# Contrast adjustment: stores issued from GpSimd's queue instead of ScalarE's

## Chip, cores, metric

One core of one Trainium2 chip. The time is the device time of one execution in microseconds (us); lower is better. Each tensor is 16 x 3 images of 512 x 512 float32 numbers, 50.33 MB, read once and written once.

## The reference

```python
mean = np.mean(x, axis=(2, 3), keepdims=True)
return np.clip(mean + factor * (x - mean), 0, 1).astype(np.float32)   # factor = 1.5
```

So the kernel computes, for each image, the sum of its pixels, and then `clip(factor * x + (1 - factor) * mean, 0, 1)`.

## The kernel before

Twelve tiles of 128 rows x 8192 columns (4.19 MB, four images each) go through a ring of six buffers in SBUF, in place. The parts that matter here:

```python
P, ROW, BUFS, SHORT, SUM = 128, 8192, 6, 2048, 4352
FIRST = (SHORT, ROW - SHORT)
# ... pools, constants, blockw: a 128 x 128 matrix that adds up the 32 rows of an image ...

def load(t, c0=0, c1=ROW, n=1):          # n tiles, columns c0 to c1, on SyncE's queue
    # ...
    nc.sync.dma_start(out=ring[:, b : b + n, c0:c1], in_=src)

def compute(t):
    xt = ring[:, t % BUFS, :]
    own = sums[:, 2 * t : 2 * t + 2]
    nc.vector.tensor_reduce(out=own[:, 0:1], in_=xt[:, 0:SUM], ...)                 # L81
    nc.scalar.activation(out=junk, in_=xt[:, SUM:ROW], func=Act.Copy, accum_out=own[:, 1:2])  # L84
    shift = bias[:, t : t + 1]
    nc.tensor.matmul(shift, blockw, own[:, 1:2], start=True, stop=False)            # L86
    nc.tensor.matmul(shift, blockw, own[:, 0:1], start=False, stop=True)            # L87
    c = 0
    for n in FIRST if t == 0 else [ROW]:
        part = xt[:, c : c + n]
        nc.vector.tensor_scalar(out=part, in0=part, scalar1=factor, scalar2=shift, ...)   # L91: x * factor + shift
        nc.vector.tensor_scalar(out=part, in0=part, scalar1=0.0, scalar2=1.0, ...)        # L94: clip
        store(t, c, c + n)
        c += n

def store(t, c0, c1):
    nc.scalar.dma_start(out=dram(out_f, t, c0, c1), in_=ring[:, t % BUFS, c0:c1])   # L101

load(0, c1=SHORT); load(0, c0=SHORT); load(1); load(2, n=2); load(4, n=2)
for t in range(n_tiles):
    compute(t)
    if t + BUFS < n_tiles:
        load(t + BUFS)          # waits until the store of tile t has landed
```

Of the kernel before, what the change touches and what calls it, by code (L numbers as in the profile page):

```python
# [1 line left out]

# [4 lines left out]


P = 128  # L10
ROW = 8192
BUFS = 6
SHORT = 2048
FIRST = (SHORT, ROW - SHORT)
SUM = 4352


@with_exitstack
def kernel(
    ctx: ExitStack,  # L20
    tc: tile.TileContext,
    x: bass.AP,
    factor: float,
    out: bass.AP,
):



    nc = tc.nc
    f32 = mybir.dt.float32  # L30
    Alu = mybir.AluOpType
    Act = mybir.ActivationFunctionType

    B, C, H, W = x.shape
    n_img, n_pix = B * C, H * W
    ppi = n_pix // ROW
    per_tile = P // ppi
    n_tiles = n_img // per_tile
    assert ppi * ROW == n_pix and per_tile * n_tiles == n_img

    factor = float(factor)
    wconst = (1.0 - factor) / float(n_pix)

    x_f = x.rearrange("b c h w -> (b c h w)")
    out_f = out.rearrange("b c h w -> (b c h w)")

    def dram(ap, t, c0=0, c1=ROW):
        return bass.AP(tensor=ap.tensor, offset=t * P * ROW + c0, ap=[[ROW, P], [1, c1 - c0]])

    consts = ctx.enter_context(tc.tile_pool(name="consts", bufs=1))  # L50
    xpool = ctx.enter_context(tc.tile_pool(name="xpool", bufs=1))
    small = ctx.enter_context(tc.tile_pool(name="small", bufs=1))
    psum = ctx.enter_context(tc.tile_pool(name="psum", bufs=1, space=bass.MemoryType.PSUM))


    sums = small.tile([P, 2 * n_tiles], f32, name="sums")
    junk = small.tile([P, ROW - SUM], f32, name="junk")
    bias = psum.tile([P, n_tiles], f32, name="bias")

    blockw = consts.tile([P, P], f32, name="blockw")  # L60
    nc.gpsimd.memset(blockw, 0.0)  # L61
    for a in range(0, P, ppi):
        nc.gpsimd.memset(blockw[a : a + ppi, a : a + ppi], wconst)  # L63


    ring = xpool.tile([P, BUFS, ROW], f32, name="ring")

    def load(t, c0=0, c1=ROW, n=1):

        b = t % BUFS  # L70
        src = bass.AP(
            tensor=x_f.tensor,
            offset=t * P * ROW + c0,
            ap=[[ROW, P], [P * ROW, n], [1, c1 - c0]],
# [6 lines that stand above are left out]
        nc.vector.tensor_reduce(  # L81
            out=own[:, 0:1], in_=xt[:, 0:SUM], axis=mybir.AxisListType.X, op=Alu.add
# [8 lines that stand above are left out]
            nc.vector.tensor_scalar(  # L91
                out=part, in0=part, scalar1=factor, scalar2=shift, op0=Alu.mult, op1=Alu.add
            )
            nc.vector.tensor_scalar(  # L94
                out=part, in0=part, scalar1=0.0, scalar2=1.0, op0=Alu.max, op1=Alu.min
            )
            store(t, c, c + n)
            c += n

    def store(t, c0, c1):  # L100
        nc.scalar.dma_start(out=dram(out_f, t, c0, c1), in_=ring[:, t % BUFS, c0:c1])  # L101

    with tc.manual_schedule():
        load(0, c1=SHORT)
        load(0, c0=SHORT)
        load(1)
        load(2, n=2)
        load(4, n=2)
# [3 lines that stand above are left out]
                load(t + BUFS)  # L112


# [1 line left out]
_INS = ['x', 'factor']  # L116
_OUTS = [((16, 3, 512, 512), 'float32')]

_NUMBERS = {'factor': 1.5}


# [26 lines left out]
```

## Time and profile before

| | before |
|---|---|
| time, median | 239.31 us (239.30 to 239.37, 3 runs) |
| span of the profiled run | 237.3 us |
| DMA queues, share of 16 engines | loads 49.7%, stores 49.2% |
| VectorE / ScalarE / GpSimd busy | 163.1 / 43.2 / 0.9 us |
| HBM traffic over the span | 424 GB/s |

How to read it: an engine's busy time is set against the span, and the two queue shares add up, because both queues feed the same 16 DMA engines. Here they add up to 98.9%: the DMA engines are the bound, and VectorE at 69% is not. The rows themselves are shown in the prediction.

### The profile page before, as it was taken

The page shows a single profiled execution, that of the slowest core. Times are in us where ns is not written, and L with a number is a line of the kernel's source. Part 1 is how long each engine was busy: PE and PEld are TensorE (multiplying, and loading weights), DVE is VectorE, ACT ScalarE, POOL GpSimd, SP SyncE. Part 2 cuts the span into 40 slices and gives each one's busy share as a digit, 9 for nine tenths or more (in the row PEclk, how much of TensorE's full clock was granted, in tenths as well). Part 3 has the DMA queues.
Part 4 walks back from the last instruction along what each step waited for, and adds up shares of the span by engine and source line. Part 5 has one row for each costly group of instructions (what it writes and reads, how often), then busy time and mean ns, then how long its engine had stood idle before and what let it go on. Part 6 is the DMA issues. An engine that isn't in the chain of part 4 may idle for free.

```text
span 237.3 us, 285 instructions
## 1 busy us (share of the span) xinstructions
PE 14.1 (6%) x48; PEld 12.0 (5%) x48; DVE 163.1 (69%) x38; ACT 43.2 (18%) x25; POOL 0.9 (0%) x9
## 2 busy tenths in 40 slices
PE   0010010001010001010010100100100100010000
PEld 0010010001010001010010100100100100010000
DVE  0079989048989328999989898891892795687000
ACT  2050230041050023050320504101400500500000
POOL 1000000000000000000000000000000000000000
DMA  7999999999999999999999999999999999999996
GB/s 297 410 442 442 421 442 359 456 439 441 442 436 414 403 431 442 442 442 442 436 442 436 414 409 425 442 442 442 442 436 442 436 420 403 425 442 442 442 442 265
DMA packets 3712, 100.66 MB, mean 424 GB/s; under 512 B 384, under 2 KB 384, under 8 KB 384
## 3 DMA queue, kind: packets, MB, share of 16 engines
q1 hardware_dynamic: 1840, 50.33, 49.7%
q10 hardware_dynamic: 1872, 50.33, 49.2%
HBM read 50.33 MB, written 50.33 MB: 424 GB/s over the span
## 4 chain that ended last, share of the span: by engine, by line
DMA 57%; DVE 29%; another core or an unknown queue 3%; PE 1%; SPq 1%; issue 0%; DVEq 0%
DMA ring<-in_x_dram 41%; DMA out_dram<-ring 16%; DVE sums L81 10%; DVE ring L91 9%; DVE ring L94 9%; PE bias L87 1%; SPq L76 1%; DVEq L91 0%
## 5 line engine op out<-in xcount | busy, mean ns | idle before, releaser
L81 DVE TENSOR_REDUCE sums<-ring 128x1 f32<-128x4352 f32 x12 | 56.2, 4683 | 45.7 <-DMA ring<-in_x_dram 45.7
L84 ACT ACTIVATE junk<-ring 128x3840 f32<-128x3840 f32 x12 | 40.8, 3403 | 163.3 <-DMA ring<-in_x_dram 107.5
L91 DVE TENSOR_SCALAR ring<-ring,bias 128x8192 f32<-128x8192 f32 (+2 forms) x13 | 54.1, 4163 | 8.9 <-PE bias L87 7.4
L94 DVE TENSOR_SCALAR ring<-ring 128x8192 f32<-128x8192 f32 (+2 forms) x13 | 53.3, 4099 | 0.4
L86 PE MATMUL bias<-sums,blockw 128*128 128x1 f32 x24 | 7.0, 361 | 190.8 <-ACT junk L84 190.8
L86 PEld LDWEIGHTS bias<-sums,blockw 128*128 128x128 f32 x24 | 6.0, 312 | 191.7 <-ACT junk L84 175.2
L87 PE MATMUL bias<-sums,blockw 128*128 128x1 f32 x24 | 7.0, 363 | 4.3 <-DVE sums L81 3.9
L87 PEld LDWEIGHTS bias<-sums,blockw 128*128 128x128 f32 x24 | 6.0, 311 | 5.3 <-DVE sums L81 5.0
L84 ACT ACTIVATION_READ_ACCUMULATOR junk<-ring 128x1 f32 x12 | 2.2, 186 | 0.0
L84 ACT ACT_TABLE_LOAD x1 | 1.3, 1283 | 0.7 <-PEq L129 0.7
L63 POOL MEMSET blockw<- 32x32 f32 x4 | 0.5, 117 | 0.2
L61 POOL MEMSET blockw<- 128x128 f32 x1 | 0.2, 204 | 0.3 <-POOLq L129 0.3
L129 POOL MEMSET const-bfloat16-1.0<- 128x1 bf16 x1 | 0.1, 111 | 0.0
L129 POOL MEMSET const-uint8-127<- 128x1 uint8 x1 | 0.1, 111 | 0.0
L129 POOL MEMSET const-float32-1.0<- 128x1 f32 x1 | 0.1, 108 | 0.0
L129 POOL MEMSET const-float32-0.0<- 128x1 f32 x1 | 0.1, 103 | 0.2 <-issue 0.2
## 6 DMA issues: line engine op xcount, KB each, us to landing
out_dram<-ring ACTq DMA_DIRECT2D x11, 4096.0 KB, 35.8
ring<-in_x_dram SPq DMA_DIRECT2D x7, 4096.0 KB, 49.7
ring<-in_x_dram SPq DMA_DIRECT2D x2, 8192.0 KB, 66.7
ring<-in_x_dram SPq DMA_DIRECT2D x1, 3072.0 KB, 11.7
out_dram<-ring ACTq DMA_DIRECT2D x1, 3072.0 KB, 28.2
ring<-in_x_dram SPq DMA_DIRECT2D x1, 1024.0 KB, 4.8
out_dram<-ring ACTq DMA_DIRECT2D x1, 1024.0 KB, 17.5
```

The source lines that it names most:

```text
L61: nc.gpsimd.memset(blockw, 0.0)
L63: nc.gpsimd.memset(blockw[a : a + ppi, a : a + ppi], wconst)
L76: nc.sync.dma_start(out=ring[:, b : b + n, c0:c1], in_=src)
L81: nc.vector.tensor_reduce(out=own[:, 0:1], in_=xt[:, 0:SUM], axis=mybir.AxisListType.X, op=Alu.add)
L84: nc.scalar.activation(out=junk, in_=xt[:, SUM:ROW], func=Act.Copy, accum_out=own[:, 1:2])
L86: nc.tensor.matmul(shift, blockw, own[:, 1:2], start=True, stop=False)
L87: nc.tensor.matmul(shift, blockw, own[:, 0:1], start=False, stop=True)
L91: nc.vector.tensor_scalar(out=part, in0=part, scalar1=factor, scalar2=shift, op0=Alu.mult, op1=Alu.add)
L94: nc.vector.tensor_scalar(out=part, in0=part, scalar1=0.0, scalar2=1.0, op0=Alu.max, op1=Alu.min)
L129: nc = _bacc.Bacc("TRN2", target_bir_lowering=False, num_devices=1)
```

## The change

The intent is to free ScalarE. A ScalarE store has to wait until VectorE has clipped the tile, and in the trace ScalarE's sum for the next tile waited behind it: 55.8 us in five waits for L94. GpSimd has little else to do (0.9 us busy).

```diff
     def store(t, c0, c1):
-        nc.scalar.dma_start(out=dram(out_f, t, c0, c1), in_=ring[:, t % BUFS, c0:c1])
+        nc.gpsimd.dma_start(out=dram(out_f, t, c0, c1), in_=ring[:, t % BUFS, c0:c1])
```

## The prediction

The "0 to 1 us" of the first two parts held a later first byte on GpSimd, and rival (b)'s upper end of 245 us, which returns in "the others 239 to 245", held a price for the smaller pieces. The 250 us of the last part is 239.3 + 11 us of idle DMA.

Three things in it, with what was measured:

- *The lock*, which stood on no trace then: a GpSimd issue is held while VectorE runs L91 or L94 (1.8 elements per ns), and not during a reduce (0.93 per ns). In the changed kernel the first issue took 3.14 us and ended 0.11 us after L91; the other 12, with a reduce or nothing after the clip, took 0.53 us. The runs show the hold and not its cause.
- *DMA starts at 2.5*: in the trace of the kernel before the first load packet started at 1.7 us and tile 0 had landed by 12.9.

> **What bounds the kernel now.** I read the page from the top: busy shares, the slices, the queues, the groups, and last the DMA issues.
>
> ```profile
> PE 14.1 (6%) x48; PEld 12.0 (5%) x48; DVE 163.1 (69%) x38; ACT 43.2 (18%) x25; POOL 0.9 (0%) x9
> ...
> DMA  7999999999999999999999999999999999999996
> ...
> q1 hardware_dynamic: 1840, 50.33, 49.7%
> q10 hardware_dynamic: 1872, 50.33, 49.2%
> ```
>
> No compute engine is near full, and the DMA row is 9 in every slice but the first and the last. The two queues (q1 the loads from SyncE, q10 the stores from ScalarE) fill 98.9% of the 16 engines' time. Measured by stretch (columns: stretch and its length, busy time and count of PE, PEld, DVE, ACT and POOL, clock, DMA share, GB/s):
>
> ```profile
> 2.00:20.00 18.00, 1.15 (x4) 1.01 (x4) 6.33 (x3) 3.52 (x3) 0.00 (x0) 1.00 1.02 433
> 20.00:36.00 16.00, 1.18 (x4) 1.00 (x4) 15.21 (x5) 3.50 (x2) 0.00 (x0) 1.00 0.99 418
> ...
> 120.00:200.00 80.00, 5.87 (x20) 5.01 (x20) 64.11 (x15) 14.22 (x10) 0.00 (x0) 1.00 1.00 433
> ```
>
> Loads alone run at 433 GB/s, and so does the mixed steady part. One transfer of a 4.19 MB tile therefore costs 4.19/0.433 = 9.7 us; 24 of them are 232.5 us, which is 98% of the 237.3 us span. So the time can move only if the engines transfer more slowly, or if they run out of work. Whether they can run dry is seen at the end (start, length, instruction):
>
> ```profile
> 203.76 4.69 DVE L81 TENSOR_REDUCE sums<-ring 128x1 f32<-128x4352 f32 x1 [4.98 <-DMA ring<-in_x_dram]
> ...
> 209.18 4.49 DVE L91 TENSOR_SCALAR ring<-ring,bias 128x8192 f32<-128x8192 f32 x1 [0.74 <-PE bias L87]
> 213.71 4.43 DVE L94 TENSOR_SCALAR ring<-ring 128x8192 f32<-128x8192 f32 x1
> 218.17 0.34 ACTq L101 DMA_DIRECT2D out_dram<-ring  x1
> ```
>
> The last load lands at 203.7; its tile needs 4.69 + 0.74 + 4.49 + 4.43, with two small hand-overs 14.4 us; its store is issued at 218.17 and the span ends at 237.3. That store alone needs 9.7 us but took 18.3 to land (the DMA view cut to the end of the span), so another 8.6 us of older stores lay ahead of it. This backlog is what hides the last 14.4 us of compute: **the kernel has 8.6 us of slack, and it consists of stores that are late.**
>
> Who gets the engines when loads and stores compete? The issues show it (KB each, median us from issue to landing):
>
> ```profile
> out_dram<-ring ACTq DMA_DIRECT2D x11, 4096.0 KB, 35.8
> ...
> out_dram<-ring ACTq DMA_DIRECT2D x1, 3072.0 KB, 28.2
> ...
> out_dram<-ring ACTq DMA_DIRECT2D x1, 1024.0 KB, 17.5
> ```
>
> The first store has rows of 8 KB, eight per engine, while the loads have rows of 32 KB. If the two queues shared by bytes, 1 MB would be through in 2 x 2.4 = 5 us. If they take turns row by row, each of its 8 rows waits for a load row: 8 x (0.3 + 1.2) = 12 us plus the start behind what is already in flight, near the 17.5 seen. (A 32 KB row takes 9.7/8 = 1.2 us of one engine.) So these two queues alternate one row each.
>
> [...] No trace here shows a GpSimd DMA.
> [...] L91 does 8192 elements in 4.49 us, 1.8 per ns, and the reduce 4352 in 4.69, 0.93 per ns. Only L91 and L94 run at the double rate.
> [...]
>
> **The change part by part.** *Removed from ScalarE:* 13 issues of 0.34 us, and the in-order wait in front of them:
>
> ```profile
> ACT junk L84 <- DVE ring L94: 55.8, 5, 11.7
> ...
> DVE ring L91 <- PE bias L87: 7.4, 10, 0.8
> ...
> PE bias L87 <- DVE sums L81: 3.9, 7, 0.6
> ```
>
> ScalarE's sum waits five times for the previous tile's last VectorE operation because the store sits in between. After the change it can start as soon as its tile has landed. That is worth nothing: its sum (3.40 + 0.19 us) already ends before VectorE's reduce (4.69), and the bias waits for the reduce. The instruction orders of PE, VectorE and SyncE do not change; only 13 issues move from ScalarE to GpSimd, which is idle (0.9 us busy).
> *Added on GpSimd:* [...] A store becomes ready when L94 ends; the next VectorE operation is a reduce or nothing, so about 5.4 us (4.69 + 0.7) are free of the lock. Only the first, short store (ready at 20.9, followed directly by L91 and L94 of the other part until 27.6) can be held, up to 6.7 us, at a time when loads fill the engines anyway. Sum of these two parts on the end: 0 to 1 us, with 8.6 us of slack above it.
> *Moved: the turns.* This is the part that can cost. Suppose a GpSimd store takes eight rows to a load's one. It then lands some 11 us after issue instead of 35.8. Every transfer given to a store early is taken from a load, and I follow that tile by tile: a transfer is 9.7 us, compute 14.4 us, 1.3 us from compute's end to first byte, DMA starts at 2.5, loads 2+3 and 4+5 are pairs.
> - Loads 0 and 1 land at 12 and 22; compute ends at 27.5 and 42. Stores 0 and 1 go first, so pair 2+3 lands after 4 loads and 2 stores, at 61 (now 50.7).
> - Tiles 2 and 3 end at 76 and 90; pair 4+5 lands after 6 loads and 3 stores, at 90. Tiles 4 and 5 end at 105 and 119.
> - Load 6 lands after 7 + 5 transfers at 119, load 7 after 8 + 7 at 148, load 8 at 158, load 9 after 10 + 8 at 177. Tiles 6 to 9 end at 134, 163, 177.5, 192.
> - Store 9 (ready at 193.5) cuts in before load 10, which lands after 11 + 10 transfers at 206.5; load 11 at 216. Tiles 10 and 11 end at 221 and 235.7.
> - No store is left when load 11 lands: the DMA idles from 216 to 222.5 (store 10), and from 232.3 to 237. Store 11 ends at 246.7.
> Idle: 6.4 + 4.7 = 11 us, where now there is none. As 100.66 MB must pass either way, the time becomes 239.3 + 11 = 250. The same count with only two rows per store turn idles 7.8 us: 247. The 8.6 us of late stores is not kept in any case.
>
> **The rivals.**
> (a) *One row per turn on GpSimd's queue too.* Then the order of transfers is today's, the latency hides in the slack, and the time is 239 to 241. For it: the hardware queues do so[...]. [...]
> (b) *Rows cut into smaller pieces.* The loads then win, the backlog of stores grows, and the end stays saturated. [...] Nothing in the profile speaks for it.
> (c) *The lock starves the stores.* For it: VectorE spends 107 us in L91 and L94. Against it: the reduce follows each L94. Even if every store waited a whole L91 and L94 (9 us), only the last could show, and after the last L94 VectorE is idle. 239 to 241.
> (d) *ScalarE's freedom pays.* Excluded above: the DMA never waits for ScalarE.
>
> **How the range and the chances follow.** I give store precedence 55%, rival (a) with (c) 33%, (b) 12%. Precedence gives 247 to 250, the others 239 to 245, mostly under the 2% line at 244.1. I take 246.5, nearer the likelier group. The range must hold both: 238.7 to 251. Slower 0.56, same 0.42; faster 0.02, since at 98% of the transfer time 2% (4.8 us) is more than the DMA has left to give.
>
> **What would show it right or wrong.** Right: time from issue to landing of the 4 MB stores near 11 to 13 us, load landings later (VectorE's third reduce at about 61, not 50.7), DMA slices under 9 near 216 to 222 and 232 to 237, ScalarE's waits for L94 gone, its busy time unchanged. If stores still land in some 36 us and the DMA row is full to the end, (a) holds and the time is about 239.5. More and smaller packets on the store queue would mean (b). A wait of L91 for something on GpSimd, or stores that start only when L94 of the next tile ends, would mean (c). A lower DMA rate in full slices would break the premise that only the order changes.

## The result, and the profile after

| | before | after |
|---|---|---|
| time, median of 6 runs | 239.28 us (239.15 to 239.37) | 239.38 us (239.21 to 240.05) |
| ratio | | 1.0011 (95% interval 0.9997 to 1.0025) |
| span of the profiled run | 237.3 us | 237.7 us |

The ratios here are formed from fast runs alone, with the kernel before as 1; they are not quite the ratios of the medians quoted.

The time did not move; 246.5 us had been predicted. The page of the changed kernel, first its busy shares, queues and DMA issues:

```profile
PE 14.0 (6%) x48; PEld 12.0 (5%) x48; DVE 163.1 (69%) x38; ACT 43.2 (18%) x25; POOL 10.4 (4%) x22
...
DMA  7999999999999999999999999999999999999996
...
q1 hardware_dynamic: 1840, 50.33, 49.6%
q0 software_dynamic: 1872, 50.33, 49.1%
...
out_dram<-ring POOLq DMA_DIRECT2D x11, 4096.0 KB, 40.8
```

The stores now go through a queue called software_dynamic, with the same 1872 packets and the same bytes as before. (The profile counts each of the 1664 rows as a packet, and one small packet more for each store on each engine: 1664 + 13 x 16 = 1872. With the 11 loads, (13 + 11) x 16 makes the 384 packets under 512 B that the page counts.) The DMA row is as full as before. And the last line settles the main question of the prediction: a store takes 40.8 us from issue to landing. The prediction had said 11 to 13 us if a GpSimd store took its rows in one turn, and some 36 if it took one row per turn.

The turns can be read off directly. This is the DMA view of the changed kernel cut to 33 to 39 us, while the first store (8 KB rows) competes with loads of 32 KB rows (first the rate in 40 slices of 0.15 us, then packets, MB and share of each queue):

```profile
GB/s 1420 1365 492 218 218 0 0 0 328 328 1201 1584 492 218 218 0 0 0 273 382 1201 1584 492 218 218 0 0 0 218 437 983 1584 655 273 0 218 0 0 218 328
...
q1 hardware_dynamic: 64, 2.10, 80.9%
q0 software_dynamic: 62, 0.51, 20.0%
```

The packet counts are equal, 64 against 62, while the bytes are four to one. The kernel before shows the same at 30 to 36 us, with its ScalarE queue:

```profile
q1 hardware_dynamic: 64, 2.10, 81.1%
q10 hardware_dynamic: 64, 0.52, 20.6%
```

Equal counts alone would also fit turns of two rows each. The rate excludes that: its peaks lie ten slices, so 1.5 us, apart, which is the time of one load row and one short store row (the prediction's 1.2 + 0.3 us; the packets of this trace took 1.21 and 0.31). So a turn is one packet, here one row, on all three queues. What did change is seen in the waits of the changed kernel (total us, times, longest), set against the same rows in the prediction:

```profile
POOL out_dram L101 <- DVE ring L94: 204.1, 13, 21.1
ACT junk L84 <- DMA ring<-in_x_dram: 159.6, 10, 29.0
...
DVE ring L91 <- PE bias L87: 7.4, 10, 0.8
```

ScalarE no longer waits for L94 (55.8 us before); GpSimd waits in its place. ScalarE's freed time became waiting for loads, and VectorE's wait for the bias is 7.4 us in both kernels: nothing was gained from it. Last, the end of the changed kernel's timeline:

```profile
200.04 4.68 DVE L81 TENSOR_REDUCE sums<-ring 128x1 f32<-128x4352 f32 x1 [4.98 <-DMA ring<-in_x_dram]
...
214.71 0.53 POOL L101 DMA_DIRECT2D out_dram<-ring  x1 [18.82 <-DVE ring L94]
```

The last load lands 3.7 us earlier than before (200.0 against 203.8) and the last store is issued 3.5 us earlier (214.7 against 218.2), yet the span is not shorter. The DMA engines have the same bytes to move and were full already: what the loads gained, the stores lost. The timeline also shows one odd thing, at the first store (start, length, instruction):

```profile
20.95 3.42 DVE L91 TENSOR_SCALAR ring<-ring,bias 128x6144 f32<-128x6144 f32 x1
21.34 3.14 POOL L101 DMA_DIRECT2D out_dram<-ring  x1 [19.75 <-DVE ring L94]
...
28.07 0.53 POOL L101 DMA_DIRECT2D out_dram<-ring  x1 [3.59 <-DVE ring L94]
```

The first issue took 3.14 us and ended at 24.48, 0.11 us after L91 ended at 24.37. The second took 0.53.

### The profile page after: what moved, and what is told of

Read it like the earlier page. It is cut to its first block, busy times and chain, and to the rows that moved or that the text cites. A ratio compares the mean times of both kernels' runs of the same rounds, so it can differ in the third digit from the quotient of the medians.

```text
span 237.7 us, 295 instructions
## 1 busy us (share of the span) xinstructions
PE 14.0 (6%) x48; PEld 12.0 (5%) x48; DVE 163.1 (69%) x38; ACT 43.2 (18%) x25; POOL 10.4 (4%) x22
## 3 DMA queue, kind: packets, MB, share of 16 engines
q0 software_dynamic: 1872, 50.33, 49.1%
## 4 chain that ended last, share of the span: by engine, by line
DMA 56%; DVE 17%; issue 12%; another core or an unknown queue 3%; PE 1%; SPq 1%; POOLq 0%; POOL 0%; DVEq 0%
DMA ring<-in_x_dram 38%; DMA out_dram<-ring 18%; DVE sums L81 6%; DVE ring L91 6%; DVE ring L94 6%; PE bias L87 1%; SPq L76 1%; POOLq L143 0%; POOL out_dram L101 0%; DVEq L91 0%; POOLq L101 0%
## 5 line engine op out<-in xcount | busy, mean ns | idle before, releaser
L84 ACT ACTIVATE junk<-ring 128x3840 f32<-128x3840 f32 x12 | 40.8, 3404 | 159.6 <-DMA ring<-in_x_dram 159.6
L91 DVE TENSOR_SCALAR ring<-ring,bias 128x8192 f32<-128x8192 f32 (+2 forms) x13 | 54.1, 4164 | 8.9 <-PE bias L87 7.4
L94 DVE TENSOR_SCALAR ring<-ring 128x8192 f32<-128x8192 f32 (+2 forms) x13 | 53.3, 4099 | 0.4
L101 POOL DMA_DIRECT2D out_dram<-ring x13 | 9.5, 733 | 204.1 <-DVE ring L94 204.1
## 6 DMA issues: line engine op xcount, KB each, us to landing
out_dram<-ring POOLq DMA_DIRECT2D x11, 4096.0 KB, 40.8
```

The lines of the kernel that those rows point to most:

```text
L101: nc.gpsimd.dma_start(out=dram(out_f, t, c0, c1), in_=ring[:, t % BUFS, c0:c1])
```

## The experiments

The theory after the result: (1) a GpSimd store takes its turns one row at a time, as a ScalarE store does, so the order of transfers stays and with it the backlog of late stores at the end; (2) this backlog is slack, and GpSimd's later start (its issues ended 0.83 us after L94 did, ScalarE's 0.37) only changes its size; (3) the 3.14 us is VectorE's lock, so L91 held the issue until it ended. Rivals are named at each run. Ten kernels ran, all with the right result. The times before in the same chip sessions were 239.14 to 239.25 us.

### Is the long first issue a lock or a start-up cost?

Tile 0 stored whole, so that no double-rate VectorE operation follows a ready store:

```diff
-        for n in FIRST if t == 0 else [ROW]:
+        for n in [ROW]:
```

> The changed kernel with tile 0 stored whole, so that no double-rate VectorE operation follows a ready store. In the changed kernel the first store's issue on GpSimd took 3.14 us, the others 0.53. Theory (VectorE's double-rate operation locks GpSimd out until it ends): all 12 issues take 0.5 to 0.6 us. Rival (the first DMA of a program on GpSimd has a start-up cost): the first issue still takes about 3.1 us. Time for both: within 0.5% of the kernel before, perhaps 0.3% under it[...].

Measured: all 12 issues took 0.53 to 0.67 us. Its timeline, GpSimd alone:

```profile
27.64 0.67 POOL L101 DMA_DIRECT2D out_dram<-ring  x1 [26.05 <-DVE ring L94]
41.94 0.53 POOL L101 DMA_DIRECT2D out_dram<-ring  x1 [13.63 <-DVE ring L94]
```

So there is no start-up cost of 3 us. The time was a miss: 241.97 us (ratio 1.0103, interval 1.0088 to 1.0119; one more run, at 249.97 us, counted as slow), 1% slower and not 0.3% faster; see the twin at the end of this section.

Then the opposite, every tile in two parts:

```diff
-        for n in FIRST if t == 0 else [ROW]:
+        for n in FIRST:
```

> The changed kernel with every tile clipped and stored in two parts (2048 and 6144 columns), so that each first part becomes ready just as a double-rate operation of 3.4 us begins. Lock theory: 12 of the 24 issues on GpSimd take about 3.1 us, the other 12 about 0.53. Start-up rival: one takes 3.1 us, 23 take 0.53. Time: the issue is late by 2.6 us but the queue has some 11 us of older stores ahead, so within 1% of the changed kernel by either theory (mixed row sizes may cost a little).

Measured: 241.15 us (ratio to the kernel before 1.0107, 1.0058 to 1.0157). Against the changed kernel's 239.38 us the median is 0.7% up, within the expected 1%; one of the four runs, at 244.22 us, widens the interval. GpSimd's timeline for the first two tiles:

```profile
21.19 3.14 POOL L101 DMA_DIRECT2D out_dram<-ring  x1 [19.60 <-DVE ring L94]
27.92 0.53 POOL L101 DMA_DIRECT2D out_dram<-ring  x1 [3.58 <-DVE ring L94]
35.73 3.16 POOL L101 DMA_DIRECT2D out_dram<-ring  x1 [7.28 <-DVE ring L94]
42.46 0.53 POOL L101 DMA_DIRECT2D out_dram<-ring  x1 [3.57 <-DVE ring L94]
```

Each first part, which becomes ready as a double-rate operation of 3.4 us begins, takes about 3.15 us to issue; each second part, which becomes ready before a reduce, takes 0.53. The hold repeats with the operation, so the lock theory stands and the start-up rival is out.

One rival is left by these two runs: the held issues are also those of the short stores. The run with short stores below settles it, since all its 48 stores are of that size. Of their issues 34 took 0.53 us. The other 14 took 1.9 to 4.5 us; each of them started while L91 or L94 was running and ended 0.12 us after that operation, as here:

```profile
127.14 4.43 DVE L94 TENSOR_SCALAR ring<-ring 128x8192 f32<-128x8192 f32 x1
129.75 1.93 POOL L102 DMA_DIRECT2D out_dram<-ring  x1 [10.41 <-DMA out_dram<-ring]
```

### Does row size set the share, on GpSimd's queue too?

Loads cut into four DMAs with 8 KB rows, stores left at 32 KB:

```diff
+    def cut_load(t, n=1):
+        for c in range(0, ROW, SHORT):
+            load(t, c, c + SHORT, n)
 ...
-        load(1)            # and all later loads
+        cut_load(1)
```

The 252 us below is the time before, the 11 us of idle DMA and a term for the shorter rows; that term had no trace behind it.

> The changed kernel with the loads cut into four DMAs of 8 KB rows, the stores left at 32 KB rows on GpSimd. Theory (the queues of SyncE and GpSimd take turns one row each, so row size sets the share): a store gets four times the bytes of a load per turn, lands in some 13 to 15 us instead of 40.8, the third tile's reduce starts near 61 us instead of 47.9, and the store backlog at the last load is gone, so the DMA idles about 11 us at the end; [...] the time is about 252 (248 to 254). Rival (the engines share by bytes, or a GpSimd store takes one packet of fixed size per turn, whatever the rows of the loads): landing stays near 40 us, no idle, time 241 to 242.

Measured: fast runs 251.13 and 254.37 us, two more runs at 254.91 and 255.49 counted as slow (one of them is the profiled one); ratio of the fast ones 1.0562 (1.0499 to 1.0625). In the profiled run, a slow one, stores landed after 16.5 us (13 to 15 expected), the third reduce started at 55.1 us, not 61, and the DMA share was 0.01 from 222 to 227.5 us, 0.25 from 237 to 242 and 0.63 from 216 to 222, which makes 5.4 + 3.8 + 2.2 = 11.4 us idle. Because of the spread and the slow profile I rely on the following twin, all of whose runs are fast.

The same cut with the stores on ScalarE:

> The kernel before, stores on ScalarE, with the loads cut into 8 KB rows as in the run on GpSimd that measured 254.6 us. Theory (the ScalarE queue and the GpSimd queue take their turns in the same way): stores again get about four times the loads' bytes while both wait, they land in 14 to 17 us, the DMA idles some 11 us at the end, 250 to 255 us. Rival (only GpSimd's queue is served that way): landing near 36 us and no idle, 241 to 243.

Measured: 251.20 us (251.0 to 251.3; ratio 1.0502, 1.0487 to 1.0518), stores landing after 16.1 us. Its end by stretch (stretch and length, engines, clock, DMA share, GB/s):

```profile
205.00:218.50 13.50, 1.17 (x4) 1.00 (x4) 12.73 (x4) 3.50 (x2) 0.00 (x0) 1.00 0.98 421
218.50:224.00 5.50, 0.00 (x0) 0.00 (x0) 5.50 (x2) 0.95 (x1) 0.00 (x0) 1.00 0.22 95
224.00:233.00 9.00, 1.18 (x4) 1.00 (x4) 8.23 (x3) 2.55 (x2) 0.00 (x0) 1.00 0.95 408
233.00:238.00 5.00, 0.00 (x0) 0.00 (x0) 3.85 (x1) 0.00 (x0) 0.00 (x0) 1.00 0.25 107
```

While VectorE works on the last tiles, the DMA engines run dry twice: 0.78 x 5.5 + 0.75 x 5.0 = 8 us (11 expected). This is the picture that the prediction drew for stores that win, brought about by the row size and not by GpSimd. Both store queues behave alike in it.

The control, both sides in 8 KB rows, stores on GpSimd (the loads are cut as above, the stores so):

```diff
+        for c in range(c0, c1, SHORT):
+            nc.gpsimd.dma_start(out=dram(out_f, t, c, c + SHORT), in_=ring[:, t % BUFS, c : c + SHORT])
-        nc.gpsimd.dma_start(out=dram(out_f, t, c0, c1), in_=ring[:, t % BUFS, c0:c1])
```

> The control of the run with short load rows: loads and stores both cut into 8 KB rows, stores on GpSimd. Theory (the row size of one queue against the other sets the share; only an uneven share drains the backlog): the share is even again, the third reduce starts near 48 to 52 us, the last load lands near 205 us, the DMA does not idle while the last tile is computed, and the time carries only the cost of short rows on both sides: 244 to 248, clearly under the 254.6 of the kernel with short load rows. Rival (short load rows themselves, by their many DMAs and semaphores, cost the 15 us): 254 or more.

Measured: 244.03 us (ratio 1.0203, 1.0188 to 1.0218). From 90 to 110 us its two queues moved exactly the same:

```profile
q0 software_dynamic: 586, 4.28, 50.6%
q1 hardware_dynamic: 586, 4.28, 50.6%
```

While the last tile was computed, from 215 to 222 us, the DMA share was 1.01. So short rows cost 4.9 us here when both sides have them, about 2.4 a side as an estimate; the uneven share costs the rest of the 12 us of the run before it.

The other way round, stores in 8 KB rows and loads in 32 KB:

The 241 to 242 us below held a figure for the shorter rows.

> The changed kernel with the stores cut into four GpSimd DMAs of 8 KB rows, the loads left at 32 KB rows. Theory (one row per turn): stores get a quarter of the loads' bytes while both wait; they land in 50 to 60 us, the third tile's reduce starts near 43 us, the last load lands near 183 us instead of 200, the DMA stays full to the end and the time rises only by the cost of shorter rows[...]: 241 to 242. Rival (GpSimd packs several descriptors of a DMA into one turn): shares stay about equal or the stores win, third reduce at 48 us or later, last load near 200 or later.

Measured: the share is a quarter, as the theory says. The DMA view from 30 to 40 us:

```profile
q1 hardware_dynamic: 102, 3.34, 78.1%
q0 software_dynamic: 96, 0.79, 18.5%
```

The third reduce started at 45.7 us (43 expected), and the last load landed by 190.6 (183 expected). A store landed after 37.4 us, where 50 to 60 had been expected: a miss. And the time was 246.65 us (ratio 1.0301, 1.0279 to 1.0322), 5 us above what I expected. Part of the rest is in sight: GpSimd waited 91.6 us, in 25 waits of up to 10.4 us, for older stores to land before it issued the next (such a wait comes before the issue and is not in the landing time); the store-only stretch from 215 to 235 us ran at 421 GB/s, where the changed kernel's last 35 us ran at 434; and from 241 to 245 us the DMA share is 0.02. I did not size these one by one. The share is shown; the cost of this variant is not fully explained.

### How large is the slack, and did the change enlarge it?

The last tile is clipped four times instead of once (same result), in both kernels, which delays its store by 13.3 us:

```diff
+            for _ in range(1 + (3 if t == n_tiles - 1 else 0)):
                 nc.vector.tensor_scalar(out=part, in0=part, scalar1=0.0, scalar2=1.0, op0=Alu.max, op1=Alu.min)
```

> The kernel before with the last tile's clip done four times instead of once (the result is the same), which delays the last store by 3 x 4.43 = 13.3 us. Its last store was issued 8.2 us before the store ahead of it landed. Theory (late stores are slack that hides late compute): the first 7 to 8 us are hidden, the rest shows: 244.4 to 245.5. Rival (the last tile's compute is on the path in full): 252.6.

> The changed kernel with the same 13.3 us of extra clips on the last tile. Its last store was issued 11.6 us before the store ahead of it landed, because its loads ran 4 us earlier. Theory (moving the stores to GpSimd made the slack 2.5 to 3.4 us larger, a gain that nothing used): 241 to 243, so 2.5 to 3.4 us faster than the kernel before with the same delay. Rival (GpSimd's later start uses the slack up, or nothing changed there): as slow as the kernel before with the delay, 244.4 or more.

Measured in the same session: 245.85 us on the kernel before (ratio 1.0281, 1.0265 to 1.0296; 0.35 us above the range expected) and 242.75 us on the changed kernel (1.0148, 1.0131 to 1.0165). By stretch, first the kernel before with the delay:

```profile
216.00:226.50 10.50, 0.00 (x0) 0.00 (x0) 10.43 (x3) 0.00 (x0) 0.00 (x0) 1.00 0.93 399
226.50:232.50 6.00, 0.00 (x0) 0.00 (x0) 5.35 (x2) 0.00 (x0) 0.00 (x0) 1.00 0.00 0
```

and the changed kernel with the delay:

```profile
216.00:226.00 10.00, 0.00 (x0) 0.00 (x0) 9.93 (x3) 0.00 (x0) 0.00 (x0) 1.00 0.97 419
226.00:229.00 3.00, 0.00 (x0) 0.00 (x0) 1.68 (x1) 0.00 (x0) 0.53 (x1) 1.00 0.00 0
```

The DMA is dry for 6 us in one and for 3 us in the other. Of the 13.3 us of delay, the kernel before hides 13.3 - 6.7 = 6.6 us and the changed one 13.3 - 3.6 = 9.7 us. (Both are set against the kernel before; the changed kernel without the delay did not run in that session.) The two delayed kernels differ by 3.1 us, so the change did bring something: 3.1 us more slack. In the kernel as it is, the last tile needs none of it.

### Where does the earlier end of the loads come from?

The kernel before, with two copies on ScalarE that hold back its first store:

```diff
+            if t == 0 and c == 0:
+                for _ in range(2):
+                    nc.scalar.activation(out=junk[:, 0:n], in_=part, func=Act.Copy)
             store(t, c, c + n)
```

The rival's 0.4 us can be set against the two traces: after the end of L94 ScalarE's issues began at 0.03 us and ended at 0.37 (12 of 13), GpSimd's began at 0.30 and ended at 0.83 (12 of 13), so 0.27 and 0.46 us later.

> The kernel before (stores on ScalarE), with two copies of 2048 columns on ScalarE in front of the first store, which hold its issue back by about 3.8 us, about as long as the first store's issue on GpSimd ended late (3.5 us). Theory (the whole difference in order between the two kernels comes from that one late store): the last load lands 3 to 4 us earlier than 203.4, at 199.5 to 200.5, stores land 2 to 3 us later, as in the changed kernel, and the time stays at 239.2 to 239.5. Rival (the order differs because every GpSimd store starts about 0.4 us later): the last load lands at 202.5 to 203.5.

Measured, one round: 239.30 us (ratio 1.0005). Its last reduce started at 201.37 us, against 203.76 before and 200.04 in the changed kernel, and its 4 MB stores landed after 39.1 us, against 35.8 and 40.8. So a later first store alone makes 2.4 of the 3.7 us. The last load landed 0.9 us after the range expected and 1.1 us before the rival's, so between the two. But the edit held the store for only half the time intended:

```profile
20.90 3.85 ACT L99 ACTIVATE junk<-ring 128x2048 f32<-128x2048 f32 x2 [4.58 <-issue]
22.85 5.06 ACTq L104 DMA_DIRECT2D out_dram<-ring  x2
```

ScalarE's queue issued it at 22.85 us, as the second copy began and not after it. That is 1.9 us later than the 20.91 before, where 3.8 had been meant, and the store's first row moved at 26.6 us, against 24.6 before and 28.1 in the changed kernel. For the remaining 1.3 us there are thus two candidates: the rest of the first store's delay, which this run did not copy, and GpSimd's later start of every store. No run separates them.

### The 1% of the unsplit first tile

The twin of the first experiment, stores on ScalarE:

> The kernel before, stores on ScalarE, with tile 0 stored whole: the twin of the run of the changed kernel with tile 0 stored whole, which measured 241.97 us, 1% over the kernel before, although 0.3% under it had been expected. If the 1% belongs to the pattern of transfers (all tiles in 32 KB rows, loads and stores in step), this twin is 1% slower too: 241 to 242.5. If it belongs to GpSimd's queue, the twin stays at 238.5 to 239.5.

Measured: 240.42 us (ratio 1.0052, 1.0035 to 1.0069), between the two cases that I had set. About half of the 1% belongs to the pattern of transfers without the split, and the other half appears only on GpSimd's queue. In the run on GpSimd the stretch from 28 to 36 us, in which the first store joins, moved 328 and 369 GB/s in its two halves instead of 433, and the dips recur as later stores begin (419 GB/s from 106 to 116 us). The twin moved 295 and 492 in the same two halves, and 462 from 106 to 116 us. Why they differ, I cannot say; this stays open. No variant beat both kernels, and none was in sight: full slices already run at 433 GB/s and nothing shortens the bytes.

## Why the prediction was wrong, point by point

- **The bound: right.** Full DMA slices at 433 GB/s in both kernels, and the same bytes; the time stayed.
- **ScalarE's freedom is worth nothing: right.** Its wait for L94 is gone, and VectorE's wait for the bias is still 7.4 us.
- **The hold of GpSimd's issues: right.** The runs show it: VectorE's L91 and L94 hold off an issue, which ended 0.11 to 0.12 us after the operation, and a reduce does not. The order of VectorE's work leaves a reduce or nothing after each tile's last clip, so 12 of 13 issues took 0.53 us. The first one was held, for 3.14 us, where up to 6.7 had been allowed: it got through after L91 and did not wait for the L94 behind it. Nothing of it reached the end.
- **The step that failed:** "Suppose a GpSimd store takes eight rows to a load's one", so its whole share of an engine in one turn. It was given 55%, on grounds that no trace shows, and the point was drawn from it. The trace shows 62 store packets against 64 load packets with bytes of one to four: one row per turn, as on the other queues. Rival (a), "One row per turn on GpSimd's queue too", 239 to 241 us, is what happened. The argument for it stood in the prediction: the two queues of the kernel before alternated one row each.
- **The condition behind the step held.** Had stores won, the kernel would have slowed as drawn. With load rows a quarter as long it measured 251.2 us on ScalarE's queue, with the DMA dry twice while the last tiles were computed; an estimated 2.4 us of the 12 belong to the short rows themselves. The third reduce came at 55 to 56 us instead of the 61 reckoned for full precedence; four to one is less than eight to one.
- **The slack was a little overstated.** 8.6 us was reckoned from the last store's landing; the delayed run hides 6.6. The reckoning gave the last store 9.7 us; alone, the delayed store took 11.1 us from issue to landing, which makes 1.4 of the 2.0 us. The other 0.6 us is not explained.
- **The range held both cases, the point did not.** The measured 239.4 lies in 238.7 to 251.0, but at its low edge: that it holds the result is owed to rival (a), which had 33%, and not to the mechanism held likelier. The point stood on a premise for which the kernel's own trace offered no evidence.

## What to carry to other kernels

When the DMA engines are full from end to end, as here at 98.9%, first ask what moving the issue of a transfer to another engine does to the order of transfers, and whether that order uses up the backlog that covers the last tile's compute. Here it cost nothing; with the first tile unsplit GpSimd's queue cost 0.5% more than ScalarE's, for reasons that stay open. In these runs two queues that both had work alternated row by row, so equal rows gave equal shares (586 packets against 586), and it was a shorter row on one side (64 against 62 packets, 2.10 against 0.51 MB), not the issuing engine, that tipped them. Before you trust a premise that no trace of the kernel shows, look for what its own trace says about the nearest thing, here the packet counts of its two queues in a window in which both have work.
